# Token sums ahead of the last tile's norm in a hybrid decoder layer on one Trainium2 core

## Chip, core and metric

The kernel runs on one core of a Trainium2 chip. The metric is device time in microseconds for one execution of the whole layer. Five engines take part: TensorE (PE; its weight loads are shown as PEld), VectorE (DVE), ScalarE (ACT), GpSimd (POOL) and SyncE (SP, which here only issues DMA transfers). Each engine works through its own queue in order. An instruction that waits holds up everything behind it on the same engine; engines meet only at semaphores, and so do the DMA transfers.

## What is computed

One layer of a decoder over 1,024 tokens plus 16 meta tokens, model width 1,024, feed-forward width 4,096, float32:

```python
for l in range(DEPTH):                                   # DEPTH = 1
    u = rmsnorm(h, g_pre_mix[l])
    z = u @ w_in[l]
    q, k, v, xr, yr = jnp.split(z, split_at, axis=-1)
    attn = sliding_window_attention_with_sinks(q, k, v, attn_sinks[l])
    xr = causal_depthwise_conv(xr, conv_w[l], conv_b[l])
    hr = rg_lru(xr, ...)
    rec = jax.nn.gelu(yr) * hr
    mix = jnp.concatenate([attn, rec], axis=-1) @ w_out[l]
    h = h + rmsnorm(mix, g_post_mix[l])
    u = rmsnorm(h, g_pre_ffn[l])
    f = jnp.square(jax.nn.relu(u @ w_ff1[l])) @ w_ff2[l]
    h = h + rmsnorm(f, g_post_ffn[l])
return h[:, N_META:]
```

The change touches the place where the output projection (`@ w_out`) ends and the first feed-forward product (`u @ w_ff1`) begins.

## The kernel before

Every float32 product is made of three matmuls (`mm3`, L123 to L133): each operand is split into a high part, rounded to the matmul's format by a copy on ScalarE (L96), and a low part, the rest, from a subtraction on VectorE (L99). `split` (L94) issues both. The three matmuls stand at L125 (high by high), L130 and L131. For a product of a weight tile and a token tile, the third needs the weight's low part and the second that of the tokens, or the other way round. In a row such as `ps_acc<-b,e` the first name is the token operand, the second the weights.

Tiles live in seven pools of equal buffers (`raw` 2, `ws` 5, `a` 16, `b` 17, `c` 8, `d` 4, `e` 2). `slot(tag, ...)` asks for one. A new tile in a pool waits until the last readers of the buffer's former tile are done; so the choice of a pool decides what a load waits for. `a` holds most of the output weights `wo` until the last output projection has been made.

The order on each engine is decided when the program is built: a scheduler takes the calls of the code with their dependences and priorities and may move independent work past each other. `behind(name, ins)` adds an order without a wait. `mark[0]` is the name of the last low part issued.

**Output projection and norms.** Tokens come in eight tiles of 128, `t` = 0 to 7. For each tile `out_mm` makes the projection, `out_norm` (L965) the norm and the residual sum (L972 squares on ScalarE, L978 and L981 on VectorE, the store L982 from SP, L984 the square of the result on ScalarE, L170 and L176 the root on GpSimd), `out_scale` the scaling (L991, VectorE). `u2_tiles` (L994) turns a scaled tile with eight transposes on TensorE (L1003), in two groups of four, and moves them from PSUM to the feed-forward's token operand `u2f`: the first group on ScalarE (L1014, four activations), the second on VectorE (L1008, two operations). Tiles 0 to 3 are half 0 of `u2f`; tiles 4 to 7 are half 1, with its columns in that order.

**Feed-forward, first product.** It is done by seven block products instead of eight (Strassen's scheme, in Winograd's form): weights and tokens are cut into blocks `11`, `12`, `21`, `22`, and sums of blocks are multiplied. The weights come in sixteen stages `p` of 256 columns. `prep_a(p)` loads both halves of a stage (L1026, two transfers of 512 KB from SP's queue, `r0` in pool `raw`, `r1` in `d` or `a`), makes four sums on VectorE (L1029), splits them into `ws` and `e` tiles and stores the last sum to `s_dram` (L1082) from GpSimd's queue. For the first stages some parts of the weights are loaded early by `early` (L1086) into a `raw` tile: block 11 of stages 0 to 3 and block 12 of stages 0 to 3, in pairs. `p1` and `p2` (L1144, L1149) are the two products that need no sum; `p1`'s result is copied on ScalarE (L1147), `p2`'s added on VectorE (L1152). The token sums are `t3` = half-1 block differences and `t2` = `t3` plus half 0 (`t_sums`), with their split operands `ot2` and `ot3`. The products of stage `p` with `ot2` and `ot3` are copied on ScalarE (L1226, L1232). `activate` (L1129) does Relu and Square (L1131, L1132) on a finished block.

**The order around the change.** After the loop over the eight tiles come `p1(0)`, `p1(1)`, `p2(0)`, `p2(1)`; then the token sums of the first three tiles of half 1 in one go (`t_sums(slice(0, 3 * P))`, 768 elements per partition and operation), `prep_a(0)`, the transposes of tile 7, the sums of its columns, `p1(2)`, `p1(3)`, the early load of block 12 for stages 2 and 3 with `p2(2)`, and from there the loop over the sixteen stages: product with `ot2`, `p1(p+2)`, product with `ot3`. `p2(3)` follows the first product with `ot2`. The scheduler puts the transposes of tiles 6 and 7 between matmuls of these products.

Of the kernel before, what the change touches and what calls it, by code (L numbers as in the profile page):

```python
# [11 lines left out]
AF = mybir.ActivationFunctionType  # L12
ALU = mybir.AluOpType
# [3 lines left out]
P = 128  # L17
# [20 lines left out]
def hybrid_layer(  # L38
# [6 lines left out]
    nc = tc.nc  # L45
# [12 lines left out]
    def slot(tag, shape, dt=F32):  # L58
        uid[0] += 1
        return slab.tile(shape, dt, tag=tag, name=f"{tag}{uid[0]}", bufs=bufs[tag])  # L60

    def pair(tag, shape):
        return slot(tag, shape, F32R), slot(tag, shape, F32R)

    def bank(tag, shape=(P, 512)):
        uid[0] += 1
        return ps.tile(list(shape), F32, tag=tag, name=f"ps_{tag}{uid[0]}")

    def f32(ap):
        return ap.bitcast(F32)  # L70
# [23 lines left out]
    def split(hi, lo, src, eng=None):  # L94
        if eng is None:
            nc.scalar.copy(hi, src)  # L96
        else:
            eng.tensor_copy(hi, src)
        low = nc.vector.tensor_tensor(lo, src, f32(hi), op=ALU.subtract).ins  # L99
        mark[0] = low.name  # L100
        return low


    mark = [None]

    def behind(name, *inss):
        for ins in inss:
            tc.add_manual_dep(
                ins, name,
                mybir.DependencyInfo(  # L110
                    mybir.DependencyClass.NoSync, mybir.DependencyReason.DATA
                ),
                reason="order",
            )
# [806 lines left out]
    u2f = [[slot("c", [P, 16, 2, 32]) for _ in range(4)], [None] * 4]  # L921
# [43 lines left out]
    def out_norm(t, po):  # L965
        xr = slot("d", [P, D])
        nc.sync.dma_start(xr, x[t * P : (t + 1) * P, :])
        h = slot("raw", [P, D])
        ssq = [small.tile([P, 1], F32, name=f"sq{n}", tag=f"sq{n}") for n in range(2)]
        for n in range(2):  # L970
            c = slice(512 * n, 512 * n + 512)
            nc.scalar.activation(  # L972
                h[:, c], po[n], AF.Square, scale=RMS_SC, accum_out=ssq[n]
            )
        rs = rstd_of(ssq)
        for n in range(2):
# [4 lines left out]
        summed[t] = nc.vector.tensor_tensor(h, h, xr, op=ALU.add).ins.name  # L981
        nc.sync.dma_start(out[t * P : (t + 1) * P, :], h)  # L982
        ssq2 = small.tile([P, 1], F32, name="ssq", tag="ssq")
        nc.scalar.activation(xr, h, AF.Square, scale=RMS_SC, accum_out=ssq2)  # L984
        return h, xr, rstd_of([ssq2])
# [8 lines left out]
    def u2_tiles(t, xn):  # L994
        half = t // 4
        if u2f[half][0] is None:
            u2f[half] = [slot("c", [P, 2, 512]) for _ in range(4)]
        o = (t % 4) * P
        for k4 in range(0, KC, 4):
            pt = bank("o", (P, 4, P))  # L1000
            for i in range(4):
                kc = k4 + i
                nc.tensor.transpose(pt[:, i, :], xn[:, kc * P : (kc + 1) * P], ident)  # L1003
            for i in range(0, 4, 2):
                kc = k4 + i
                dst = u2f[half][kc // 2]
                if k4:
                    nc.vector.tensor_tensor(  # L1008
                        dst[:, :, o : o + P], pt[:, i : i + 2, :],
                        g_ffn_col[:, kc : kc + 2].to_broadcast([P, 2, P]), op=ALU.mult,  # L1010
                    )
# [16 lines left out]
    def combine(dst, x0, x1, op):  # L1028
        return nc.vector.tensor_tensor(dst, x0, x1, op=op).ins  # L1029

    def rows(t_, c=slice(0, 512)):
        if len(t_.shape) == 4:
            return t_[:, c.start // 32 : c.stop // 32]
        return t_[:, :, c].rearrange("p k (g t) -> p g k t", t=32)
# [48 lines left out]
        return first, (hl[:, 0], hl[:, 1]), (hi[:, :, HI], lo[:, :, HI])  # L1083


    def early(b, p0, hl):  # L1086
        raw = slot("raw", [P, 2, 4, P])
        for k in range(2):
            w1_load(raw[:, k], b, p0 + k, 0, 1)
        split(*hl, raw)  # L1090
        return {p0 + k: (hl[0][:, k], hl[1][:, k]) for k in range(2)}

    a11_early, a12_early = {}, {}
# [34 lines left out]

    def activate(k, q):  # L1129
        t_ = fb[k][q]  # L1130
        nc.scalar.activation(t_, t_, AF.Relu)  # L1131
        return nc.scalar.activation(t_, t_, AF.Square).ins  # L1132

    pos = [out_banks(t) for t in range(4)]
# [7 lines left out]
    ESH = [P, 2, 4, P]  # L1142
# [6 lines left out]
    def p2(p, w, after=None):  # L1149
        y2 = bank("pt")  # L1150
        product(y2, w, b21, True, after)
        nc.vector.tensor_tensor(block("11", p), y2, block("11", p), op=ALU.add)  # L1152

    for t in range(8):
        po = pos[t] if t < 4 else out_banks(t)
        out_mm(t, po, range(6 if t < 4 else 0, KC))
        if t > 5:
            u2_tiles(t - 2, xns[t - 2])
        halfway[t] = out_norm(t, po)
        for k in scale_at[t]:  # L1160
            xns[k] = out_scale(k, *halfway.pop(k))
        if 1 <= t <= 4:
            u2_read(t - 1)
        if t == 7:
            u2_tiles(6, xns[6])
        if t == 4:
            a11_early.update(early(0, 0, pair("a", ESH)))
        if t == 5:
            b11 = operand(u2f[0][0:2])
            a12_early.update(early(1, 0, pair("ws", ESH)))  # L1170
        if t == 6:
            b21 = operand(u2f[0][2:4])
            hl = slot("b", ESH, F32R), slot("e", ESH, F32R)
            a11_early.update(early(0, 2, hl))

    for p in range(2):
        p1(p, a11_early[p])
    for p in range(2):
        p2(p, a12_early[p])
    t3 = [slot("a", [P, 2, 512]) for _ in range(2)]  # L1180
    t2 = [slot("a", [P, 2, 512]) for _ in range(2)]
    ot2 = [pair("b", [P, 2, 512]) for _ in range(2)]

    def t_sums(c):
        for i in range(2):
            combine(t3[i][:, :, c], u2f[1][2 + i][:, :, c], u2f[1][i][:, :, c], ALU.subtract)
            combine(rows(t2[i], c), rows(t3[i], c), rows(u2f[0][i], c), ALU.add)
            hi, lo = ot2[i]
            split(hi[:, :, c], lo[:, :, c], t2[i][:, :, c])

    t_sums(slice(0, 3 * P))
    wa[0] = prep_a(0)
    u2_tiles(7, xns[7])
    t_sums(slice(3 * P, 4 * P))
    urgent = mark[0]
    for p in range(2, 4):
        p1(p, a11_early[p])
    a12_early.update(early(1, 2, pair("a", ESH)))
    p2(2, a12_early[2])
    ot3 = [pair("b", [P, 2, 512]) for _ in range(2)]  # L1200
    for i in range(2):
        behind(urgent, split(*ot3[i], t3[i]))
    wa[1] = prep_a(1, urgent)


# [351 lines left out]
```

## Time and profile before

| | us |
|---|---|
| median of 3 runs (lowest to highest) | 953.0 (952.5 to 953.69) |
| the profiled execution, its own time | 953.17 |
| its span in the profile | 951.5 |
| TensorE busy | 939.7 |
| VectorE busy | 664.5 |
| ScalarE busy | 503.3 |
| GpSimd busy | 135.3 |

The granted TensorE clock is full (0.999) over the span. Times in the views below are microseconds from the start of the span. A row of a timeline gives start, duration, engine, line, operation, tile written and tiles read (without buffer numbers), shape, how many in a row, and in brackets the idle time of the engine before it and what ended it. A row with "x2" shows the duration of both together. TensorE's matmuls are pipelined: each lasts 0.39 us in the record and the next starts while it is under way, so distances between starts matter, not durations. "SPq" rows are the issue of transfers, not the transfers. In the view of waits a row gives the waiting engine, tile and line, who released it, the sum, the number and the longest of such waits. In the windows a row gives, for a stretch of the span, its length, then busy time and number of instructions of PE, PEld, DVE, ACT and POOL, the granted clock, the DMA share and GB/s.

### The profile page before, as it was taken

The numbers are of one execution on the slowest core, as the hardware profiler recorded it, in microseconds if no ns is written. First come the engines' busy times: TensorE is split into PE (matmuls) and PEld (weight loads), VectorE is DVE, ScalarE is ACT, GpSimd is POOL, SyncE is SP. The second block draws the span as 40 slices with busy tenths as digits, with TensorE's granted clock in tenths as the row PEclk, the third lists the DMA queues.
The fourth block names the chain that finished last, engine by engine and source line by source line (L and its number), as shares of the span: only waits on it lengthen the run. The fifth ranks groups of instructions, "written<-read, shape, count | busy, mean of one in ns | idle before, by whom it ended". The sixth has DMA issues, their size and how long they took to land.

```text
span 951.5 us, 12169 instructions
## 1 busy us (share of the span) xinstructions
PE 939.7 (99%) x4584; PEld 785.5 (83%) x4584; DVE 664.5 (70%) x845; ACT 503.3 (53%) x838; POOL 135.3 (14%) x205
## 2 busy tenths in 40 slices
PE   9999999999999999999999999999999999999996
PEld 8999999878888877888888888888888888888885
DVE  6667788779977877665644465476667676779783
ACT  7546765569634554443655585654533343445441
POOL 4104437430021100010000000000121000001201
PEclk9999999999999999999999999999999999999999
DMA  8220011104258567674422364334777755537934
GB/s 272 57 67 23 24 45 45 45 23 145 77 198 267 192 202 243 205 236 148 167 91 89 111 200 131 96 111 127 199 160 179 204 187 186 194 129 210 233 65 89
DMA packets 97366, 134.91 MB, mean 142 GB/s; under 512 B 22230, under 2 KB 61158, under 8 KB 97308
## 3 DMA queue, kind: packets, MB, share of 16 engines
q1 hardware_dynamic: 87996, 108.64, 35.1%
q0 software_dynamic: 8880, 24.19, 12.0%
q10 hardware_dynamic: 432, 1.31, 0.4%
q8 instruction: 36, 0.59, 0.3%
q14 instruction: 22, 0.18, 0.1%
HBM read 112.55 MB, written 20.97 MB: 140 GB/s over the span
## 4 chain that ended last, share of the span: by engine, by line
PE 95%; DMA 2%; DVE 2%; ACT 0%; issue 0%; SPq 0%; DVEq 0%
PE ps_acc L125 11%; PE ps_acc L130 11%; PE ps_acc L131 11%; PE ps_pt L131 6%; PE ps_pt L125 6%; PE ps_pt L130 6%; PE ps_s L131 6%; PE ps_s L125 6%; PE ps_s L130 6%; PE ps_o L125 5%; PE ps_o L130 5%; PE ps_o L131 5%; PE ps_o L697 2%; PE ps_acc L282 1%; PE ps_s L629 1%; PE ps_s L633 1%
## 5 line engine op out<-in xcount | busy, mean ns | idle before, releaser
L99 DVE TENSOR_TENSOR ws<-raw,ws 128x1024 fp32r<-128x1024 f32 (+1 forms) x69 | 82.3, 1193 | 71.3 <-PE ps_o L130 23.1
L96 ACT CAST ws<-raw 128x1024 fp32r<-128x1024 f32 (+1 forms) x68 | 69.7, 1026 | 83.6 <-PE ps_o L130 33.6
L96 ACT CAST ws<-e 128x1024 fp32r<-128x1024 f32 x41 | 43.0, 1049 | 85.6 <-PE ps_o L130 38.2
L130 PE MATMUL ps_acc<-a,ws 128*128 128x512 f32 (+3 forms) x240 | 83.0, 346 | 0.0
L125 PE MATMUL ps_acc<-a,ws 128*128 128x512 f32 (+3 forms) x240 | 82.8, 346 | 0.0
L131 PE MATMUL ps_acc<-a,ws 128*128 128x512 f32 (+3 forms) x240 | 82.2, 343 | 0.0
L99 DVE TENSOR_TENSOR b<-b,b 128x1024 fp32r<-128x1024 f32 (+2 forms) x50 | 59.0, 1179 | 27.9 <-PE ps_o L130 22.7
L96 ACT CAST b<-b 128x1024 fp32r<-128x1024 f32 (+2 forms) x49 | 50.0, 1020 | 42.1 <-DVE b L1029 35.8
L99 DVE TENSOR_TENSOR ws<-e,ws 128x1024 fp32r<-128x1024 f32 x41 | 50.2, 1224 | 30.4 <-ACT ws L96 17.1
L684 POOL TENSOR_SCALAR_AFFINE_SELECT c<-c 128x512 fp32r<-128x512 f32 x64 | 55.0, 873 | 73.7 <-ACT c L96 64.2
L125 PEld LDWEIGHTS ps_acc<-a,ws 128*128 128x128 f32 x240 | 45.2, 189 | 4.3 <-issue 0.7
L131 PEld LDWEIGHTS ps_acc<-a,ws 128*128 128x128 f32 x240 | 45.2, 188 | 3.7 <-issue 0.2
L130 PEld LDWEIGHTS ps_acc<-a,ws 128*128 128x128 f32 x240 | 45.2, 188 | 3.6 <-issue 0.4
L131 PE MATMUL ps_acc<-ws,b 128*128 128x512 f32 (+1 forms) x120 | 46.3, 386 | 0.0
L130 PE MATMUL ps_acc<-ws,b 128*128 128x512 f32 (+1 forms) x120 | 46.2, 385 | 0.0
L125 PE MATMUL ps_acc<-ws,b 128*128 128x512 f32 (+1 forms) x120 | 46.0, 385 | 0.0
L125 PE MATMUL ps_pt<-ws,b 128*128 128x512 f32 x112 | 44.3, 395 | 0.0
L131 PE MATMUL ps_pt<-ws,b 128*128 128x512 f32 x112 | 44.2, 395 | 0.0
L130 PE MATMUL ps_pt<-ws,b 128*128 128x512 f32 x112 | 44.1, 394 | 0.0
L130 PE MATMUL ps_s<-ws,b 128*128 128x512 f32 x110 | 43.4, 395 | 0.0
L131 PE MATMUL ps_s<-ws,b 128*128 128x512 f32 x110 | 43.4, 394 | 0.0
L125 PE MATMUL ps_s<-ws,b 128*128 128x512 f32 x110 | 43.4, 394 | 0.0
(417 smaller groups left out, 2660.3 us busy)
## 6 DMA issues: line engine op xcount, KB each, us to landing
raw<-in_w_ff_dram SPq DMA_DIRECT2D x59, 512.0 KB, 3.9
e<-in_w_ff_dram SPq DMA_DIRECT2D x43, 512.0 KB, 3.2
a<-in_w_ff_dram SPq DMA_DIRECT2D x12, 512.0 KB, 4.9
s_dram<-a POOLq DMA_DIRECT2D x12, 512.0 KB, 3.9
raw<-in_w_in_dram SPq DMA_DIRECT2D x9, 512.0 KB, 3.6
c<-in_x_dram SPq DMA_DIRECT2D x8, 512.0 KB, 5.2
d<-in_x_dram SPq DMA_DIRECT2D x8, 512.0 KB, 3.2
out_dram<-raw SPq DMA_DIRECT2D x8, 512.0 KB
```

The costliest lines, as they stand in the source:

```text
L96: nc.scalar.copy(hi, src)
L99: low = nc.vector.tensor_tensor(lo, src, f32(hi), op=ALU.subtract).ins
L125: ins = nc.tensor.matmul(dst, lh, rh, start=start, stop=False, skip_group_check=True).ins
L130: nc.tensor.matmul(dst, lh, rl, start=False, stop=False, skip_group_check=True)
L131: last_mm[0] = nc.tensor.matmul(dst, ll, rh, start=False, stop=stop, skip_group_check=True).ins.name
L282: last_mm[0] = nc.tensor.matmul(acc[:, :n], w[k // 2][:, kc, :], u[kc][k % 2][:, t0 : t0 + n], start=k == 0 and kc == 0, stop=k == last an ...
L629: nc.tensor.matmul(dst, q[h][:, c], hi, start=True, stop=False, skip_group_check=True,)
L633: nc.tensor.matmul(dst, q[h][:, c], lo, start=False, stop=True, skip_group_check=True,)
L684: nc.gpsimd.affine_select(out=p_[:, :, s], in_=f32(p_[:, :, 0]), pattern=[[0, 4], [g, P]], compare_op=op, fill=0.0, base=0, channel_multip ...
L697: nc.tensor.matmul(two[:, :, oc : oc + w], v, p_.rearrange("p (j i) s c -> p j (i s c)", j=2)[:, :, pc : pc + w], start=n == 0 and k == 0, ...
```

## The change

```diff
@@ u2_tiles
-                if k4:
+                if k4 and t != 6:
                     nc.vector.tensor_tensor(
                         dst[:, :, o : o + P], pt[:, i : i + 2, :],
                         g_ffn_col[:, kc : kc + 2].to_broadcast([P, 2, P]), op=ALU.mult,
@@
-    def early(b, p0, hl):
-        raw = slot("raw", [P, 2, 4, P])
+    def early(b, p0, hl, tag="raw"):
+        raw = slot(tag, [P, 2, 4, P])
@@ activate
-        nc.scalar.activation(t_, t_, AF.Relu)
+        ins = nc.scalar.activation(t_, t_, AF.Relu).ins
+        if k == "11":
+            behind(token_low, ins)
         return nc.scalar.activation(t_, t_, AF.Square).ins
@@
+    def t_sums(c):
+        for i in range(2):
+            combine(t3[i][:, :, c], u2f[1][2 + i][:, :, c], u2f[1][i][:, :, c], ALU.subtract)
+            combine(rows(t2[i], c), rows(t3[i], c), rows(u2f[0][i], c), ALU.add)
+            hi, lo = ot2[i]
+            split(hi[:, :, c], lo[:, :, c], t2[i][:, :, c])
+
     for t in range(8):
...
         if t > 5:
             u2_tiles(t - 2, xns[t - 2])
+        if t == 7:
+            t3 = [slot("a", [P, 2, 512]) for _ in range(2)]
+            t2 = [slot("a", [P, 2, 512]) for _ in range(2)]
+            ot2 = [pair("b", [P, 2, 512]) for _ in range(2)]
         halfway[t] = out_norm(t, po)
...
         if t == 7:
+            t_sums(slice(0, 2 * P))
             u2_tiles(6, xns[6])
@@
+    a12_early.update(early(1, 2, pair("a", ESH), "a"))
     for p in range(2):
         p1(p, a11_early[p])
     for p in range(2):
         p2(p, a12_early[p])
-    t3 = [slot("a", [P, 2, 512]) for _ in range(2)]
-    t2 = [slot("a", [P, 2, 512]) for _ in range(2)]
-    ot2 = [pair("b", [P, 2, 512]) for _ in range(2)]
-
-    def t_sums(c):
-        ...
-    t_sums(slice(0, 3 * P))
+    t_sums(slice(2 * P, 3 * P))
     wa[0] = prep_a(0)
     u2_tiles(7, xns[7])
     t_sums(slice(3 * P, 4 * P))
     urgent = mark[0]
     for p in range(2, 4):
         p1(p, a11_early[p])
-    a12_early.update(early(1, 2, pair("a", ESH)))
     p2(2, a12_early[2])
     ot3 = [pair("b", [P, 2, 512]) for _ in range(2)]
     for i in range(2):
         behind(urgent, split(*ot3[i], t3[i]))
+    token_low = mark[0]
     wa[1] = prep_a(1, urgent)
```

Four things, then. The token sums of tiles 4 and 5 (512 elements per partition and operation) are made inside the last turn of the tile loop, and those of tile 6 (256 elements) later, instead of all three in one piece. The early weights for block 12 of stages 2 and 3 are loaded before the first `p1`, into a buffer of pool `a` instead of `raw`. Relu and Square of each `11` block are ordered behind the low part of the second `ot3` operand. All eight transposes of tile 6 are evicted by ScalarE.

In the built program this also moves the order of neighbouring work. On VectorE the three sums of tiles 4 and 5 stand ahead of tile 6's scaling (L991), the fourth and the first low part ahead of L978 of tile 7, the second low part ahead of L981 of tile 7, and the low part of the early weights right behind it. On TensorE `p1(2)` is no longer interrupted; tile 6's transposes stand four matmuls later, and three matmuls instead of nine lie between tile 7's transposes and `p2(2)`. In SP's queue the early load stands ahead of `r0` of stage 0; `r1` of stage 2 follows that directly; and `r1` of stages 5 and 6 and of 14 and 15 stand behind `r0` of stage 5 and ahead of `r0` of stage 6 (before: `r1` of 5 and 6 ahead of `r0` of 5, `r1` of 14 and 15 behind `r0` of 6). VectorE's first sum of stage 5 stands ahead of the low part of stage 4 (before: behind it). From stage 7 on the orders are the same. The number of transfers and of matmuls is the same.

More of the change, by code (lines that the diff above doesn't have):

```diff
@@ L1179, in hybrid_layer @@
         p2(p, a12_early[p])
-    t3 = [slot("a", [P, 2, 512]) for _ in range(2)]
-    t2 = [slot("a", [P, 2, 512]) for _ in range(2)]
-    ot2 = [pair("b", [P, 2, 512]) for _ in range(2)]
-    def t_sums(c):
[L1185 to L1189, printed above, removed]
-    t_sums(slice(0, 3 * P))
+    t_sums(slice(2 * P, 3 * P))
     wa[0] = prep_a(0)
```

## The prediction

> **What bounds the kernel now.** I read the page first: busy times and the chain that ended last.
>
> ```profile
> span 951.5 us, 12169 instructions
> ...
> PE 939.7 (99%) x4584; PEld 785.5 (83%) x4584; DVE 664.5 (70%) x845; ACT 503.3 (53%) x838; POOL 135.3 (14%) x205
> ...
> PE 95%; DMA 2%; DVE 2%; ACT 0%; issue 0%; SPq 0%; DVEq 0%
> ```
>
> TensorE is the bound from end to end, and the change neither adds nor removes a matmul. It can only move the moments at which TensorE waits. The view of waits for TensorE lists six of them: two in the first microseconds, the other four here (the first and the last of these; all four stand with their brackets in the timeline below).
>
> ```profile
> PE ps_pt L131 <- DVE a L99: 1.0, 1, 1.0
> ...
> PE ps_acc L130 <- DVE b L99: 0.2, 1, 0.2
> ```
>
> These four lie in the change from the output projection to the first feed-forward products. The timeline of TensorE shows where, and gives their full price (start, duration, then the idle time in brackets):
>
> ```profile
> 334.32 0.39 PE L125 MATMUL ps_pt<-b,a 128*128 128x512 f32 x1
> 334.55 0.39 PE L130 MATMUL ps_pt<-b,a 128*128 128x512 f32 x1
> 335.94 0.50 PE L131 MATMUL ps_pt<-b,a 128*128 128x512 f32 x1 [1.00 <-DVE a L99]
> 336.28 0.39 PE L125 MATMUL ps_pt<-b,a 128*128 128x512 f32 x1
> ...
> 338.13 0.39 PE L131 MATMUL ps_pt<-b,a 128*128 128x512 f32 x1
> 338.96 0.50 PE L125 MATMUL ps_acc<-b,e 128*128 128x512 f32 x1 [0.44 <-ACT b L96]
> 339.70 0.50 PE L130 MATMUL ps_acc<-b,e 128*128 128x512 f32 x1 [0.24 <-DVE b L99]
> ...
> 348.93 0.50 PE L131 MATMUL ps_acc<-b,e 128*128 128x512 f32 x1
> ...
> 359.44 0.40 PE L130 MATMUL ps_s<-b,e 128*128 128x512 f32 x1
> 360.39 0.50 PE L131 MATMUL ps_s<-b,e 128*128 128x512 f32 x1 [0.56 <-DVE e L99]
> ...
> 363.34 0.50 PE L131 MATMUL ps_acc<-b,ws 128*128 128x512 f32 x1
> ```
>
> Undisturbed matmuls start 0.23 us apart (334.32 to 334.55), and after a wait the next start is 0.34 later (335.94 to 336.28), 0.11 over. So the four waits cost 335.94-334.55-0.23+0.11 = 1.27, then 0.60, 0.62 and 0.83: 3.3 us, of which 2.5 lie before 340. The matmuls at 348.93 and 363.34, both the first to use a low part, took 0.50 like those after a wait: held up too, too briefly for the list of waits, by some 0.2 each with the 0.11. **3.7 us** is the whole prize, 0.39% of the span.
>
> The windows of 5 us say why (busy time of each engine, clock, DMA share, GB/s):
>
> ```profile
> 325.00:330.00 5.00, 5.00 (x24) 4.04 (x23) 5.00 (x10) 1.79 (x5) 1.49 (x2) 1.00 0.60 168
> 345.00:350.00 5.00, 5.00 (x23) 3.80 (x22) 5.00 (x9) 4.07 (x6) 1.08 (x2) 1.00 0.20 73
> 350.00:355.00 5.00, 5.00 (x23) 4.09 (x22) 0.08 (x1) 1.18 (x2) 0.00 (x0) 1.00 0.99 291
> ```
>
> VectorE has no gap around 325 to 350, and then stands idle for 5 us behind a load. Here, and only here, VectorE's queue sets when TensorE's operands are ready.
>
> **The change part by part.** Its rows on VectorE and ScalarE:
>
> ```profile
> 318.80 0.75 DVE L991 TENSOR_SCALAR d<-raw,rs 128x1024 f32<-128x1024 f32 x1 [1.42 <-POOL rs L176]
> 321.72 1.23 DVE L981 TENSOR_TENSOR raw<-raw,d 128x1024 f32<-128x1024 f32 x1
> 326.00 0.74 DVE L991 TENSOR_SCALAR d<-raw,rs 128x1024 f32<-128x1024 f32 x1
> 334.00 0.75 DVE L1008 TENSOR_TENSOR c<-ps_o,gcol 128x256 f32<-128x256 f32 x2
> 334.67 1.22 DVE L99 TENSOR_TENSOR a<-raw,a 128x1024 fp32r<-128x1024 f32 x1
> 335.80 0.76 DVE L1029 TENSOR_TENSOR a<-c,c 128x256 f32<-128x256 f32 x2
> 336.47 0.96 DVE L99 TENSOR_TENSOR b<-a,b 128x768 fp32r<-128x768 f32 x1
> ...
> 348.19 1.29 DVE L99 TENSOR_TENSOR e<-raw,e 128x512 fp32r<-128x512 f32 x2
> ```
>
> ```profile
> 323.04 1.06 ACT L984 ACTIVATE d<-raw 128x1024 f32<-128x1024 f32 x1 [0.83 <-DVE raw L981]
> ...
> 333.94 1.08 ACT L1131 ACTIVATE d<-d 128x1024 f32<-128x1024 f32 x1
> 334.89 0.84 ACT L96 CAST b<-a 128x768 fp32r<-128x768 f32 x1
> 335.61 1.08 ACT L1132 ACTIVATE d<-d 128x1024 f32<-128x1024 f32 x1
> ```
>
> From start to start an operation on VectorE holds its queue for 0.33 us with 256 elements (335.80 to 336.47 is two), 0.60 with 512 (the two of 348.19 take 1.29, and one alone 0.69, by the row of 355.74 below), 0.87 with 768 (336.47 to the next at 337.34) and 1.13 with 1024 (334.67 to 335.80).
>
> *Token sums.* Six operations of 768 elements (5.2 us) become six of 512 (3.6) and six of 256 (2.0): 0.4 us more. The two evictions of tile 6 that go to ScalarE take off 0.67 (334.00 to 334.67). ScalarE gets them as four more activations, about 1 us, in a window where it is busy 1.79 of 5 us. VectorE's total hardly moves; the place does. VectorE idled 1.42 us before 318.80, and the three sums of tiles 4 and 5 that the new order puts there take 1.9 (one waits on its forerunner), so tile 6's scaling starts at 319.3 instead of 318.80, and tile 7's residual sum (321.72), behind three further pieces, at 323.2: 1.5 late. Who waits for it: ScalarE's square of tile 7 (323.04, now behind the copy of a product, 324.9), GpSimd's root, and VectorE's scaling of tile 7. The last starts 2.96 us after the square now (323.04 to 326.00), so at 327.5 to 327.9. TensorE wants it for tile 7's transposes:
>
> ```profile
> 331.35 1.04 PE L1003 MATMUL ps_o<-ident,d 128*128 128x128 f32 x8
> ```
>
> In the new order three matmuls instead of nine stand between these eight and the product at 334.32, so they come at 334.3-0.7-0.9 = 332.7. Cover for the late scaling: over 4 us; past that, each microsecond late is one of TensorE's.
>
> By "VectorE: DVE Perf Modes" of the Trainium skill (section on the TRN2 errata) every VectorE instruction that reads SBUF pays a fixed cost, some 150 cycles at 0.96 GHz in its measurement, so pieces should hold 512 elements or more. The rows above give 0.06 us for the fixed part (0.33 for 256, 0.60 for 512); by the page the six extra instructions would cost 0.9 us instead of 0.4, an estimate, and half a microsecond would be gone from the room that the last sums have below: the sum would be 0.2 to 0.3 us worse at most.
>
> *Early weights.* The load of the third early pair moves ahead of the first stage's second load and no longer waits in SP's queue for a `raw` buffer:
>
> ```profile
> 326.77 3.04 SPq L1026 DMA_DIRECT2D raw<-in_w_ff_dram  x3
> ...
> 348.90 1.61 SPq L1026 DMA_DIRECT2D raw<-in_w_ff_dram  x2
> 350.56 1.76 SPq L1026 DMA_DIRECT2D a<-in_w_ff_dram  x2
> 360.37 5.42 SPq L1026 DMA_DIRECT2D raw<-in_w_ff_dram  x2
> ```
>
> It was among the three at 326.77; now its buffer is free when the last output projection has ended, so it is issued at about 316.5. Its low part, at 334.67 the thing TensorE waits 1.27 us for, comes at 324.4, ten microseconds before use. It takes 0.5 MB in front of stage 0's second load (issued near 320.1), which VectorE needs by 325.5, when its queue gets there: 5.4 us against a median of 3.9:
>
> ```profile
> raw<-in_w_ff_dram SPq DMA_DIRECT2D x59, 512.0 KB, 3.9
> ```
>
> Were it later than 325.5, VectorE's whole queue would stand behind it, one for one; I take nothing.
>
> *The last tile's sums and the squares.* Relu and Square of the first block (333.94, 335.61, about 1 us each) stood between the casts; now they come behind. I laid the operations in their new order with the durations above. Transposes end at 333.6, VectorE's two evictions start at 333.8, the four sums of 256 end at 336.0, ScalarE's cast for the first operand ends between 336.3 and 336.7, its low part 0.4 later. TensorE, not stopped before, asks at 337.0 and 337.3. Both waits (0.60 and 0.62) go, with 0.2 to 0.6 us to spare.
>
> *What is late next.* TensorE runs 2.5 us earlier, VectorE, laid in the same way, ends its run at 348.4 instead of 350.1: 1.7 earlier. The product of stage 1 starts 48 matmuls after 334.3, at 345.4; its third step, two matmuls of the next product in between, at 346.3 wants a low part that VectorE has ready at 346.6: a new wait of 0.4+0.1 = **0.5**. The load of stage 3 (348.90) can be issued at 346.7, when that low part frees its buffer. Landing 5.5 us later, between 3.9 and the 6.8 shown below, it gives its operands by 356.2, before the product that needs them (48 matmuls and the 0.5 after 345.4: 356.9). The 0.83 goes as well.
>
> *The queue of SP.* In the changed order the loads for stages 5 and 6 (the pair at 350.56) no longer go out ahead of stage 5's first half; they stand behind it, and it waits for stage 3's buffer, freed with that low part at about 356.3. Five loads of 0.5 MB then leave together, with two stores of GpSimd. VectorE's first sum of stage 5, which needs two of them, is queued ahead of the low part of stage 4, wanted by TensorE 86 matmuls and the 0.5 after 345.4, at 365.7. That sum, two more operations of 512 elements and the low part itself come to 2.5 us, so both loads must have landed by 363.2. Nearest row:
>
> ```profile
> 347.97 0.55 POOL L1082 DMA_DIRECT2D s_dram<-d  x1 [19.68 <-DVE d L1029]
> 348.57 0.53 POOL L1082 DMA_DIRECT2D s_dram<-a  x1
> ...
> 355.74 0.69 DVE L1029 TENSOR_TENSOR a<-raw,a 128x512 f32<-128x512 f32 x1 [5.66 <-DMA raw<-in_w_ff_dram]
> ```
>
> The first of four loads, with two stores beside them, was there 6.8 us after its issue at 348.90. I take 7 us from the second issue, 356.8: landing at 363.8, a new wait of 0.6+0.1 = **0.7**. Bounds: nothing (5 us or less, when fewer transfers share) and 5.8 (below). Later stages have no wait in the view above, and the changed program keeps their order.
>
> **Sum**: the 3.7 all go, -3.7 + 0.5 + 0.7 = **-2.5 us**. The profiled execution took 953.17 with its span of 951.5, 0.2 above the median of 953.0: from the median, **950.5**.
>
> **Rivals.** A, the transfer is not late: the first two of the five loads land within 6.4 us of issue, the 0.7 vanishes: 949.8. For it: the median of 3.9; against it: 6.8 at 355.74, with fewer transfers. "DMA: Bandwidth & Descriptors" of the Trainium skill (section on queues, rings and completion order) says that a ring's descriptors are consumed in order; by that rule loads behind cannot slow the first, and A's time would follow. The trace leaves it open, since GpSimd's stores ran beside.
>
> B, both groups are slow: stage 3's load, too, takes 6.8 us, so its low part and stage 4's weights are late by 0.2 and 0.9, and the group of five takes 7 to 8 us from there (0.9 to 1.9): with the 0.5, waits of 2.5 to 3.5 against 3.7 removed: 951.8 to 952.8.
>
> C, the change does not do what it says: tile 7's chain slips by over a microsecond (GpSimd's root, ScalarE's order), and the 0.60 and 0.62 stay: 951.7. Against it: 4 us of cover for the scaling; for it: 0.2 us at the end.
>
> D, slower: the same wait of VectorE's queue at stage 5, with the second load landing only as the whole group is through. Five loads and two stores are 3.7 MB, at the 291 GB/s of 350 to 355 us 12.6 us: 368.9, 5.7 us late, 5.8 of wait: 955.6. It decides from a landing after 366.4, where 3.2 us of wait eat all that is left of the gain.
>
> **How the numbers follow.** Forecast 0.40 (own range 950.0 to 951.1), A 0.22, B 0.20, C 0.08, D 0.10. A measurement of this kernel tells about 0.2%, 1.9 us, from no change: under 951.1 is faster, over 954.9 slower. Faster: forecast, A and an edge, 0.64; slower 0.09, since a part of D stays within; same 0.27. The range 949.6 to 952.8 takes A, the forecast, C and nearly all of B.
>
> **What would show it.** Right: no wait on `a` L99 at p2(2), none on `b` at the first product of the sums; one on `e` L99 near 346 and one near 366; VectorE waiting for a load at about 357 to 364. Wrong: waits on `b` near 337 (C), a VectorE gap reaching past 366 (D), none near 366 (A).

## The result and the profile after

| | before | after |
|---|---|---|
| median (lowest to highest), us | 952.81 (952.5 to 953.69, 6 runs) | 949.15 (948.88 to 949.59, 6 runs) |
| the profiled execution, its own time | 953.17 | 949.03 |
| its span | 951.5 | 947.3 |

The ratio is 0.9961, 95% interval 0.9948 to 0.9974: 3.7 us faster. The prediction had the sign, but the time lies 0.45 us below its range. The page of after begins like that of before:

```profile
span 947.3 us, 12174 instructions
...
PE 937.9 (99%) x4584; PEld 784.8 (83%) x4584; DVE 664.4 (70%) x849; ACT 505.0 (53%) x844; POOL 135.9 (14%) x205
```

The number of matmuls and VectorE's total are as before. The view of waits for TensorE has only the two of the first microseconds left:

```profile
PE ps_acc L309 <- DVE base_e L563: 1.5, 1, 1.5
PE ps_o L358 <- DVE d L248: 0.6, 1, 0.6
```

**Two accounts.** I went through TensorE's timeline from 311 to 400 us and added up what each distance between starts exceeds the undisturbed pace (0.231 us for a matmul of 512 columns, 0.099 for a transpose). This *excess* is 3.97 us before and 0.70 after, so the place of the change gave **3.27 us**. In both, some 0.27 of it stands behind three groups of transposes, which the change does not remove; without them 3.7 became 0.43. What is left after is one short hold (start, duration, operation):

```profile
345.13 0.48 PE L125 MATMUL ps_s<-b,e 128*128 128x512 f32 x1
345.45 0.40 PE L130 MATMUL ps_s<-b,e 128*128 128x512 f32 x1
345.92 0.51 PE L131 MATMUL ps_acc<-b,e 128*128 128x512 f32 x1
346.26 0.40 PE L125 MATMUL ps_acc<-b,e 128*128 128x512 f32 x1
```

The distances 0.32, 0.47 and 0.34 are 0.09, 0.24 and 0.11 over the pace: stage 1's low part, which the prediction had put at 0.5.

The other account is the time up to the change. The chain of waits starts at the first load of the input in both profiles (start and duration); before, then after:

```profile
1.71 5.13 DMA c<-in_x_dram
```

```profile
1.71 4.50 DMA c<-in_x_dram
```

That load landed 0.63 us sooner in the profiled execution of after, and the lead lasted: one and the same matmul, the second of a product just ahead of the change, starts at 316.11 before and at 315.35 after. So 0.76 of the 4.2 us between the two spans arose in code that the change doesn't touch (3.27 + 0.76 = 4.03). Times of after below are therefore compared with those of the prediction by adding 0.76.

VectorE of after, the rows that answer to the prediction's steps (bracket: idle time before and what ended it):

```profile
318.46 0.75 DVE L991 TENSOR_SCALAR d<-raw,rs 128x1024 f32<-128x1024 f32 x1 [0.46 <-POOL rs L176]
...
322.32 1.22 DVE L981 TENSOR_TENSOR raw<-raw,d 128x1024 f32<-128x1024 f32 x1
323.45 1.22 DVE L99 TENSOR_TENSOR a<-a,a 128x1024 fp32r<-128x1024 f32 x1
...
326.76 0.76 DVE L991 TENSOR_SCALAR d<-raw,rs 128x1024 f32<-128x1024 f32 x1 [0.76 <-POOL rs L176]
...
335.63 0.42 DVE L99 TENSOR_TENSOR b<-a,b 128x256 fp32r<-128x256 f32 x1 [0.47 <-ACT b L96]
...
345.18 0.69 DVE L99 TENSOR_TENSOR e<-raw,e 128x512 fp32r<-128x512 f32 x1
345.78 0.69 DVE L1029 TENSOR_TENSOR a<-a,raw 128x512 f32<-128x512 f32 x1
...
346.98 0.69 DVE L99 TENSOR_TENSOR e<-raw,e 128x512 fp32r<-128x512 f32 x1
350.87 0.69 DVE L1029 TENSOR_TENSOR a<-raw,a 128x512 f32<-128x512 f32 x1 [3.20 <-DMA raw<-in_w_ff_dram]
...
361.28 0.69 DVE L1029 TENSOR_TENSOR a<-raw,a 128x512 f32<-128x512 f32 x1 [1.34 <-DMA a<-in_w_ff_dram]
...
363.09 0.69 DVE L99 TENSOR_TENSOR e<-raw,e 128x512 fp32r<-128x512 f32 x1
```

SP's issues of after, and the first two matmuls of stage 4's product, which the forecast stall would have held up at the second low part:

```profile
315.73 1.12 SPq L1026 DMA_DIRECT2D a<-in_w_ff_dram  x2
...
345.89 9.45 SPq L1026 DMA_DIRECT2D raw<-in_w_ff_dram  x3
355.39 1.71 SPq L1026 DMA_DIRECT2D a<-in_w_ff_dram  x2
357.14 1.58 SPq L1026 DMA_DIRECT2D d<-in_w_ff_dram  x2
```

```profile
364.80 0.40 PE L130 MATMUL ps_acc<-b,e 128*128 128x512 f32 x1
365.04 0.40 PE L131 MATMUL ps_acc<-b,e 128*128 128x512 f32 x1
```

The second of the five loads (one at the end of the x3, then the two pairs) is issued at 355.39 and ends VectorE's wait at 361.28: it landed in 5.9 us, not 7. Stage 4's low part (363.09) is done at 363.78, and TensorE asks for it at 365.04. The stall that the prediction priced at 0.7 did not come, with 1.26 us to spare.

### The profile page after: what moved, and what is told of

It is laid out like the page before. It is cut to its first block, busy times and chain, and to the rows that moved or that the text cites. A ratio compares the mean times of both kernels' runs of the same rounds, so it can differ in the third digit from the quotient of the medians.

```text
span 947.3 us, 12174 instructions
## 1 busy us (share of the span) xinstructions
PE 937.9 (99%) x4584; PEld 784.8 (83%) x4584; DVE 664.4 (70%) x849; ACT 505.0 (53%) x844; POOL 135.9 (14%) x205
## 4 chain that ended last, share of the span: by engine, by line
PE 97%; DVE 1%; DMA 0%; ACT 0%; issue 0%; SPq 0%; DVEq 0%
PE ps_acc L125 12%; PE ps_acc L131 12%; PE ps_acc L130 12%; PE ps_pt L131 6%; PE ps_s L131 6%; PE ps_pt L125 6%; PE ps_pt L130 6%; PE ps_s L125 6%; PE ps_s L130 6%; PE ps_o L125 5%; PE ps_o L131 5%; PE ps_o L130 5%; PE ps_o L697 2%; PE ps_acc L282 1%; PE ps_s L629 1%; PE ps_s L633 1%
```

## The experiments

All runs beside the kernel before on the same chip. "Matmul" is the start of that matmul ahead of the change in the profiled execution (a measure of how late the start was), "excess" is TensorE's as above, up to 372 us and from there to 400. The last column is 953.0 minus 3.97 plus the excess, what the time would be if nothing else differed from the kernel before. The kernel before itself had medians of 952.81 to 953.21 us beside them, so the ratios compare better across rows than the medians.

| run | median, us | ratio [95%] | matmul | excess to 372 / to 400 | by the excess |
|---|---|---|---|---|---|
| before | 953.0 | 1 | 316.11 | 3.97 / 0 | 953.0 |
| after, first | 949.15 | 0.9961 [0.9948, 0.9974] | 315.35 | 0.70 / 0 | 949.7 |
| r1 after again | 950.25 | 0.9968 [0.9956, 0.9981] | 315.44 | 0.69 / 0 | 949.7 |
| u1 sums in one piece | 952.04 | 0.9989 [0.998, 0.9998] | 315.47 | 2.80 / 0 | 951.8 |
| u2 weights as before | 951.97 | 0.9989 [0.998, 0.9998] | 315.80 | 2.86 / 0 | 951.9 |
| u3 squares as before | 952.34 | 0.9994 [0.9985, 1.0002] | 316.73 | 2.87 / 0 | 951.9 |
| u4 tile 6 as before | 951.81 | 0.9988 [0.9979, 0.9997] | 315.64 | 2.61 / 0 | 951.6 |
| b1 weights alone | 951.92 | 0.9986 [0.9977, 0.9994] | 315.68 | 3.17 / 0.27 | 952.5 |
| f1 three loads | 951.20 | 0.9981 [0.9972, 0.999] | 316.73 | 0.68 / 1.25 | 951.0 |
| f2 nine loads | 953.78 | 1.0003 [0.9994, 1.0012] | 317.51 | 0.68 / 2.93 | 952.6 |
| x1 stage 1 low first | 950.08 | 0.9964 [0.9951, 0.9976] | 316.00 | 0.85 / 0 | 949.9 |
| o1 after, write first | 951.47 | 0.998 [0.9971, 0.9989] | 315.56 | 2.36 / 0 | 951.4 |
| o2 before, load first | 952.97 | 0.9997 [0.9988, 1.0006] | 315.56 | 3.68 / 0 | 952.7 |
| o3 tile 6, load first | 951.58 | 0.9982 [0.9973, 0.9991] | 316.40 | 2.36 / 0 | 951.4 |
| o4 before, load and cast first | 951.97 | 0.9988 [0.9979, 0.9996] | 315.29 | 2.79 / 0 | 951.8 |
| o5 tile 6, load and cast first | 950.57 | 0.9972 [0.9962, 0.9982] | 315.87 | 1.42 / 0 | 950.5 |

The last column agrees with the median within 0.3 us in ten of the fifteen rows below that of before. It fails for u3 by 0.4, for b1 and the two sets of after by about 0.6, and for f2 by 1.2. The profiled executions do add up: 953.17, the time of that of before, plus the differences in excess and in the start of the matmul, gives the time of each of the other fifteen within 0.35 us. That of f2 (953.97) started 1.40 us later than that of before; whether its other executions did is not recorded.

### The same kernel again

> The changed kernel once more, unaltered, beside the others on one chip. If the 0.76 us that its profiled execution was ahead before 315 us (first load of x landed 4.50 us behind its start, 5.13 before) belongs to the execution and not to the kernel, the profiled start differs again and the median comes out at 949.1 to 949.9, 3.1 to 3.8 us below the kernel before. If it belongs to the kernel, the first load lands at 6.2 us again.

Median 950.25 (949.47 to 951.03, 5 runs): above the interval that was expected by 0.35. The kernel before had 953.21 beside it, not 952.81, so the gain is 2.96 us here and 3.66 in the first set. The excess is the same to 0.01 us. The first load landed 4.68 us after its start, neither 4.50 nor 5.13, and the matmul ahead of the change started at 315.44. This profiled execution was the fastest of the five; what made the other four 0.7 to 1.6 us slower, no trace shows. In o4, whose code up to that place is that of the kernel before, the matmul started at 315.29; in f1 and f2, whose code there is that of after, at 316.73 and 317.51. In all sixteen traces the lead or lag against after is there by 30 us and changes by less than 0.1 us from there to 315. So the start does not come from the code that the change touches. All eleven runs of after together have a median of 949.47; the two sets lie 0.3 us below it and 0.8 above.

### One part of the change undone, or done alone

u1: the sums of all three tiles in one piece, where they were.

```diff
-            t_sums(slice(0, 2 * P))
...
-    t_sums(slice(2 * P, 3 * P))
+    t_sums(slice(0, 3 * P))
```

> The changed kernel with the token sums of tiles 4, 5 and 6 made in one piece again, at their old place; the other three parts stay. Queue theory (VectorE's idle time before 323 us is what the early sums fill): the 3.6 us of sums of 512 elements fall back into the full stretch after 325, while the low part of the early weights (1.1 us) stays out of it. The low part of the third early pair now stands ahead of tile 5's evictions and waits there for its load, some 3 us. So the waits on the sums' operands near 337 come back: 1 to 2 us of waits on b in all, none on a at p2(2), and 950.2 to 951.2 for the time. Rival (the early weights alone made the gain): no wait near 337, 949.0 to 949.4.

u2: the early weights loaded into `raw`, where they were.

```diff
-    a12_early.update(early(1, 2, pair("a", ESH), "a"))
...
+    a12_early.update(early(1, 2, pair("a", ESH)))
     p2(2, a12_early[2])
```

> The changed kernel with the early weights for stages 2 and 3 loaded into a raw buffer at their old place; the other three parts stay. Queue theory: the low part (1.1 us) falls back to about 334 us, and TensorE waits for it at p2(2) as before, 1.0 to 1.3 us; the sums' operands are ready in time because TensorE asks for them that much later. Time 950.0 to 950.6. Rival (the sums alone made the gain): no wait at p2(2), 949.0 to 949.4.

u3: Relu and Square not held behind the sums.

```diff
-        if k == "11":
-            behind(token_low, ins)
```

> The changed kernel without the order of Relu and Square behind the sums' low parts; the other three parts stay. In the built order Relu and Square of the first block then stand ahead of the cast of t3, the cast for the first operand of the sums comes some 1.2 to 1.9 us later, at 336.5 to 337.5 on the changed kernel's clock, and TensorE asks at 336.3. Queue theory: a wait on b at the first product with the sums of 0.5 to 1.5 us, time 949.6 to 950.6. Rival (this order is hidden): none, 949.0 to 949.4.

u4: tile 6's second group evicted on VectorE.

```diff
-                if k4 and t != 6:
+                if k4:
```

> The changed kernel with the second group of tile 6's transposes evicted by VectorE again; the other three parts stay. VectorE gets 0.67 us more work right ahead of tile 7's scaling, where the changed kernel's VectorE stood idle for 0.76 us waiting for GpSimd's root. Queue theory: hidden to 0.3 us, waits of TensorE as in the changed kernel (0.5 us in all) or up to 0.4 more near 337, time 949.1 to 949.6. Rival (each instruction off VectorE counts in full): 0.67 more, 949.8.

b1: the kernel before, with the early weights in pool `a` alone.

```diff
+    a12_early.update(early(1, 2, pair("a", ESH), "a"))
     for p in range(2):
         p1(p, a11_early[p])
...
-    a12_early.update(early(1, 2, pair("a", ESH)))
```

> The kernel before with only the early weights moved and put into pool a; no other part. In the built order their cast and low part stand ahead of tile 5's evictions on ScalarE and VectorE and wait there some 3 us for the load. Queue theory: the 1.27 us at p2(2) go, but VectorE's run up to 350 ends little earlier, so part of it comes back as longer waits on the sums' operands near 337; TensorE's waits between 312 and 400 are 2.5 to 4.0 us (4.0 in the kernel before), time 951.3 to 952.8. Rival (each part brings its own wait's price): 951.5, with the waits on b unchanged at 1.2.

Each of the four undone alone gives back 1.9 to 2.2 us of the 3.27, so that the losses add up to 8.3; and the weights alone gain 0.5 to 1.1 us, less than the 1.27 of the wait that they remove. The parts don't add. The other three were not run alone. In b1 the wait on `a` is gone, TensorE comes earlier to the first product with the sums, and waits there for 1.18 us on ScalarE's cast instead of 0.44. In u2 that wait on `a` is back, on ScalarE's cast first. ScalarE, then TensorE of u2:

```profile
334.61 1.04 ACT L96 CAST a<-raw 128x1024 fp32r<-128x1024 f32 x1 [1.44 <-DMA raw<-in_w_ff_dram]
```

```profile
335.71 0.50 PE L125 MATMUL ps_pt<-b,a 128*128 128x512 f32 x1 [1.53 <-ACT a L96]
```

In u3 the casts of the sums stand behind the Square, as the prediction read it from the profile of before. ScalarE and TensorE of u3:

```profile
336.44 1.10 ACT L1132 ACTIVATE d<-d 128x1024 f32<-128x1024 f32 x1
337.39 2.62 ACT L96 CAST b<-a 128x1024 fp32r<-128x1024 f32 x4
```

```profile
338.82 0.50 PE L125 MATMUL ps_acc<-b,e 128*128 128x512 f32 x1 [0.93 <-ACT b L96]
```

u4 shows what the two evictions are worth. They take VectorE 0.67 us, and in u4 its queue has the addition of `p2(2)`, which waits for TensorE, ahead of the sums' last low parts; in after, one of these (335.63 above) goes in front of it. VectorE and TensorE of u4:

```profile
336.83 0.69 DVE L1154 TENSOR_TENSOR b<-ps_pt,b 128x512 f32<-128x512 f32 x1 [0.68 <-PE ps_pt L131]
337.44 1.89 DVE L99 TENSOR_TENSOR b<-a,b 128x256 fp32r<-128x256 f32 x3
```

```profile
337.91 0.50 PE L130 MATMUL ps_acc<-b,e 128*128 128x512 f32 x1 [0.82 <-DVE b L99]
```

That is 1.05 us of excess. A second loss is common to u1, u3, u4 and b1: the wait on `e` near 360, gone in after and in u2, is there with 0.5 to 0.7 us and its small neighbours. The last group of runs goes into it.

### Does a load wait for those behind it?

f1: the loads of stages 14 and 15 held back until stage 7's first, so that three loads leave together at stage 5 and not five.

```diff
+        if p > 13:
+            behind(r0_load[7], ins)
```

> The changed kernel with the loads for stages 14 and 15 ordered behind stage 7's first load: three transfers instead of five leave SP's queue when stage 3's buffer comes free. The prediction's step (loads behind slow those ahead): the second load, which VectorE waits for at 361.3, lands 1 to 2 us earlier than the 5.9 us after its issue of the changed kernel. Ring order (loads behind cannot slow the first): it lands within 0.4 us of 5.9. Either way TensorE has no wait there; the time is 949.0 to 949.4.

f2: four more transfers of 512 KB, from weights to a scratch area in DRAM that nothing reads, right behind the load in question: nine.

```diff
+        if p == 5:
+            for n in range(4):
+                more = nc.sync.dma_start(more_dram[n], w1v[0][:, :, 256 * (11 + n) : 256 * (12 + n)]).ins
+                behind(ins.name, more)
```

> The changed kernel with four more transfers of 512 KB, from the weights to unused memory, in SP's queue right behind the first two of the five loads for stages 5 and later: nine instead of five. It computes nothing more. The prediction's step: the second load lands 2 us or more later than the 5.9 us after its issue, and TensorE waits at stage 4's low part for 1 us or more. Ring order: it lands within 0.5 us of 5.9, no wait near 365; only what stands behind, the loads of stage 6, comes later, with waits there of 0 to 3 us.

SP and VectorE of f1 (the load, and the sum that waits for it), then of f2:

```profile
356.73 1.69 SPq L1026 DMA_DIRECT2D a<-in_w_ff_dram  x2
```

```profile
362.31 0.69 DVE L1029 TENSOR_TENSOR a<-raw,a 128x512 f32<-128x512 f32 x1 [0.98 <-DMA a<-in_w_ff_dram]
```

```profile
357.54 0.67 SPq L1026 DMA_DIRECT2D a<-in_w_ff_dram  x1
358.26 4.12 SPq L1069 DMA_DIRECT2D more_dram<-in_w_ff_dram  x4
...
366.42 4.12 SPq L1026 DMA_DIRECT2D raw<-in_w_ff_dram  x2
```

```profile
363.43 0.69 DVE L1029 TENSOR_TENSOR a<-raw,a 128x512 f32<-128x512 f32 x1 [1.33 <-DMA a<-in_w_ff_dram]
...
377.63 0.69 DVE L1029 TENSOR_TENSOR a<-raw,a 128x512 f32<-128x512 f32 x1 [6.35 <-DMA raw<-in_w_ff_dram]
```

From issue to the end of the wait: 5.58 us with three loads, 5.89 with five (after), 5.89 with nine. The loads behind do not slow it by more than 0.31 us, and four more cost nothing. Those behind the added transfers are late instead: VectorE idles 6.35 us at stage 6, TensorE waits 2.18 us near 380, and the kernel loses all it had gained. In f1 a wait of TensorE for ScalarE, 0.98 us, came near 389, where the order of the later loads had changed. This settles the prediction's rivals A and D. The Trainium skill, "DMA: Bandwidth & Descriptors" (section on queues, rings and completion order), says that each DMA engine takes a ring's descriptors in order; the traces agree, with 5.89 us for five loads and for nine.

### Stage 1's low part first

x1: in stage 1, the `e` operand's sum and low part ahead of the other low part, for the 0.43 us that are left.

```diff
+        if p == 1:
...
+            low = split(hl[:, 0], hl[:, 1], a11).name
+            behind(low, split(hi[:, :, HI], lo[:, :, HI], a21))
```

> The changed kernel with the low part of stage 1's sum (the e tile) made ahead of the low part of its other half (the ws tile). The wait of 0.24 us and its two delays of 0.1 near 345.9 go: TensorE's waits between 312 and 397 fall from 0.7 to 0.3, which is what the transposes show in any case. Queue theory: 0.4 us faster than the changed kernel, 948.6 to 949.0, too little to tell from it by the times alone. Rival (something else is late by as much): the wait moves to the next low part, 949.1.

The hold near 346 shrank from 0.44 to 0.30 us beyond the pace, but small ones of 0.11 and 0.18 us came back near 357 and 360; with the 0.27 of the transposes 0.85 in all. Its 950.08 can't be told from after. With 0.43 us left at this place, another order of it can gain no more than that, less than the two sets of after differ by.

### Which order brings the wait on `e` back?

In u1, u3, u4 and b1, as in the kernel before, VectorE makes stage 2's last sum ahead of stage 1's low part; in after and in u2 it is the other way round (345.18 and 345.78 above). The sum releases GpSimd's second store to DRAM; the low part frees the `raw` buffer, and so releases stage 3's load. GpSimd, SP and VectorE of u4:

```profile
346.77 0.53 POOL L1082 DMA_DIRECT2D s_dram<-a  x1
```

```profile
347.11 1.62 SPq L1026 DMA_DIRECT2D raw<-in_w_ff_dram  x2
```

```profile
353.92 0.69 DVE L1029 TENSOR_TENSOR a<-raw,a 128x512 f32<-128x512 f32 x1 [5.63 <-DMA raw<-in_w_ff_dram]
```

The load landed 6.81 us after its issue; in after 4.98 (345.89 to 350.87), with the second store issued behind it:

```profile
346.76 0.53 POOL L1082 DMA_DIRECT2D s_dram<-a  x1 [0.65 <-DVE a L1029]
```

Three runs ask for the swap of the two instructions alone. o1 puts after's into the order of before; o2 and o3 put those of before and of u4 into the order of after.

```diff
-        split(hl[:, 0], hl[:, 1], a11)
-        combine(a12, a12, a11, ALU.subtract)
+        e_low[p] = split(hl[:, 0], hl[:, 1], a11)
+        a12_sum = combine(a12, a12, a11, ALU.subtract)
+        if p == 2:
+            behind(e_low[1].name, a12_sum)
```

(In o1 the last line is `behind(a12_sum.name, e_low[1])`.)

> The changed kernel, with VectorE's low part of stage 1 (which frees a raw buffer) put behind stage 2's sum (which starts the second 512 KB write to DRAM), as the kernel before has these two; nothing else is asked for, but the order of the later loads comes back to that of the kernel before with it. In the traces so far stage 3's load landed 4.98, 4.99, 4.94, 4.97 and 4.67 us behind its issue where that lay ahead of the second write, and 6.84, 6.94, 6.79, 6.81 and 6.92 where it lay behind it. Theory (the load queues behind the write): issue some 0.6 us later, landing 6.8 to 6.9 us behind it, a wait of 0.5 to 0.8 us of TensorE at stage 3's low part near 359, and 0.5 to 0.8 us more than the changed kernel of this call. Rival (it landed early for another reason, the later order of SP's queue): landing 5.0 and no more than 0.2 us of difference.

> The kernel before with one pair of VectorE's instructions swapped: stage 1's low part ahead of stage 2's sum, so that stage 3's load is issued ahead of the second write. Theory: the load is issued 0.6 us earlier and lands 5.0 us behind its issue (6.84 before), TensorE's wait of 0.56 us on e near 360 goes, and the kernel runs 0.6 to 0.8 us faster than before (about 952.3); the waits of 1.0, 0.44 and 0.24 us at 335 to 340 stay. Rival (four loads in a bunch share the engines): it lands 6.8 us behind its issue, and the wait shrinks only by the 0.6 us of the earlier issue.

> The changed kernel with tile 6's evictions as before, and the same pair of VectorE's instructions put in the changed kernel's order (stage 1's low part ahead of stage 2's sum). Theory: of the 1.9 us that the changed kernel loses with tile 6's evictions as before, the load's part (a wait of 0.55 us at 358.6 and its small one behind it) comes back: 0.6 to 0.8 us faster than that run, 951.0 to 951.2; the wait of 0.82 us on b near 337.9 stays, since its cause is the two evictions on VectorE. Rival (the evictions cost it all): no difference.

GpSimd, SP and VectorE of o1:

```profile
346.36 0.53 POOL L1086 DMA_DIRECT2D s_dram<-a  x1
```

```profile
346.69 11.95 SPq L1026 DMA_DIRECT2D raw<-in_w_ff_dram  x3
```

```profile
353.63 0.69 DVE L1029 TENSOR_TENSOR a<-raw,a 128x512 f32<-128x512 f32 x1 [5.77 <-DMA raw<-in_w_ff_dram]
```

The landing follows the order each time: 6.94 us in o1 (346.69 to 353.63), 4.94 in o2 (347.75 to 352.69), 4.93 in o3. Two other things move with the swap. The next load in SP's queue follows 1.20 to 1.24 us behind in o1 and before, 1.80 to 1.85 in after and o2; but f1 and f2 show that a load behind matters little. And the load is issued 0.93 us behind the first store in o1, 0.33 in after; but in x1 it is 0.96, with the second store issued behind the load, and it landed in 4.67. So the second store is left. The transfers of the profile show it at work: in o1, from 346.5 to 350.5 us, the two stores' packets (1.04 MB) take 83% of the DMA engines' time, and only 0.08 MB of the load's 0.52 moves beside them; it lands 3.1 us after that.

TensorE's wait did not follow. In o1 it came back as expected, 0.63 us at 358.3, and the run cost more than expected, 1.2 us against r1 (1.67 in the excess), since the swap also made stage 1's low part 0.6 us later, for which TensorE waits already. But in o2 and o3 a wait of 0.47 us stayed, and o2 gained nothing that can be measured. VectorE and ScalarE of o2:

```profile
352.69 0.69 DVE L1029 TENSOR_TENSOR a<-raw,a 128x512 f32<-128x512 f32 x1 [3.15 <-DMA raw<-in_w_ff_dram]
...
357.02 0.69 DVE L99 TENSOR_TENSOR ws<-raw,ws 128x512 fp32r<-128x512 f32 x1 [2.19 <-ACT ws L96]
```

```profile
355.89 0.59 ACT L1236 COPY a<-ps_acc 128x512 f32<-128x512 f32 x1 [2.19 <-PE ps_acc L131]
356.37 0.62 ACT L96 CAST ws<-raw 128x512 fp32r<-128x512 f32 x1
```

The load lands 1.9 us sooner after its issue than in before, but VectorE now waits 2.19 us for the cast, and the cast stands behind an eviction that waits 2.19 us for TensorE. With the swap, the built order had taken these two the other way round (before: cast at 357.19, eviction at 357.71). o4 and o5 are o2 and o3 with that eviction behind the casts:

```diff
-        nc.scalar.copy(block("21", p), ya[p])
+        ins = nc.scalar.copy(block("21", p), ya[p]).ins
+        if p == 1:
+            behind(e_cast, ins)
```

> The kernel before with the swap of run o2 (stage 3's load ahead of the second write) and one more: ScalarE's eviction of stage 1's second product, which waits for TensorE until 355.9 us, is put behind the two casts of stage 3. In run o2 the load landed 1.9 us earlier, but the cast stood behind that eviction (cast at 356.37, its operand summed by 354.8), and TensorE's wait at stage 3's low part stayed at 0.47 us. Theory (the wait passed from the load to ScalarE's queue): casts at 354.2 to 355.5, stage 3's low part done by 357.6, asked for at 358.9; the wait of 0.47 and its small neighbours (0.64 + 0.06 beyond the pace) go, and the run is 0.6 to 0.8 us faster than o2 (952.97), so 952.2 to 952.4. Rival (VectorE's queue holds it: stage 4's sum, which stands ahead of stage 3's low part and waits for stage 4's load): the wait stays at 0.3 us or more.

> The changed kernel with tile 6's evictions as before (the load first as in run o3), and the same order on ScalarE: the eviction behind stage 3's two casts. Theory: TensorE's wait of 0.47 us at 359 goes, what stays against the changed kernel is the wait on b near 338 (0.31 + 0.75 us beyond the pace in o3, 0.05 to 0.1 in the changed kernel), and the run is 0.6 to 0.8 us faster than o3 (951.58), so 950.8 to 951.0. Rival: as in o4, no difference.

ScalarE of o4, and its waits of TensorE:

```profile
353.89 0.62 ACT L96 CAST ws<-raw 128x512 fp32r<-128x512 f32 x1 [0.40 <-DVE raw L1029]
354.61 0.62 ACT L96 CAST e<-raw 128x512 fp32r<-128x512 f32 x1
355.69 0.59 ACT L1238 COPY a<-ps_acc 128x512 f32<-128x512 f32 x1 [0.45 <-PE ps_acc L131]
```

```profile
PE ps_pt L131 <- DVE a L99: 1.0, 1, 1.0
...
PE ps_acc L125 <- ACT b L96: 0.4, 1, 0.4
PE ps_acc L130 <- DVE b L99: 0.3, 1, 0.3
```

The wait on `e` is gone in both. The excess fell by 0.89 (o2 to o4) and 0.94 us (o3 to o5), the time by 1.0 and 1.0 (951.97 after 952.97, 950.57 after 951.58; these were not run side by side, so the two figures of the traces weigh more). Shown, then: the load ahead of the store does not remove that wait by itself, and with the cast ahead of the eviction it does. The cast alone was not moved in any run; in before VectorE's row from the landing (355.74) to stage 3's low part (359.66) has no gap, and the cast that this low part reads was done 0.85 us before, so there the load held it. After has both (350.87 above; the casts of stage 3 at 352.32 and 353.05, the eviction at 353.63). What u4 loses apart from it is the 1.05 near 338, still there in o5.

## Why the prediction was right or wrong

- **TensorE as the bound, and the 3.7 us prize.** Right: without the transposes there were 3.69 us of excess before, and all but 0.2 us of the rest of the difference between the two profiles is their start.
- **The first three waits go** (1.27, 0.60, 0.62). Right, by the steps laid out. With 0.76 added: the early load issued at 316.5 (316.5 forecast), its low part at 324.2 (324.4), tile 6's scaling 319.2 (319.3), tile 7's residual sum 323.1 (323.2), its scaling 327.5 (327.5 to 327.9). Rival C fell.
- **The 0.83 goes.** Right in its result: VectorE's run ends at 348.43 (348.4) and stage 3's load is issued at 346.65 (346.7). The landing was set at 5.5, between bounds, and was 4.98; why one or the other holds was not seen. The runs showed it: whether GpSimd's second store goes first. The first half of rival B is this case with the store first: o1, with 6.94 us for stage 3's load, had 951.47. Its second half, 7 to 8 us for the group of five, came in no run (5.8 to 6.0 us in after, r1, u2 and o1).
- **A new 0.5 at stage 1's low part.** Right: 0.43 to 0.44, asked for at 346.4 (346.3 forecast) and ready at 346.6 (346.6).
- **A new 0.7 at stage 4's low part.** Wrong: this is the step that failed, "I take 7 us from the second issue, 356.8: landing at 363.8". The load was issued at 356.15 on that clock and landed 5.89 us later, at 362.04; needed by 363.2. Of the 1.76 us, 1.1 come from the landing and 0.65 from the earlier issue. The nearest row, 6.8 us at 355.74, was no measure of how many loads share a queue: it was a load behind two stores, and the prediction put two stores beside the five loads as well; in after one store (354.03) stood ahead of them, and the next was issued at 362.99, after the landing. Rival A, with 949.8, is what happened.
- **The sum.** With that term at nothing it is -3.7 + 0.43 = -3.27, measured -3.27 in the excess: 949.7 from 953.0. The two sets of after, 949.15 and 950.25, lie on either side of it. The range began 0.2 us under rival A, less than the 1.1 us between the two sets of this kernel, so that the first set fell below it.
- **Fixed cost of small pieces on VectorE.** No wait arose where the six extra instructions went; VectorE's run ended to 0.03 us where the rows' durations had put it.

## What to carry to other kernels

When loads queue on one engine, price a landing by what is ahead of it, in its own queue and in the others, and not by what is behind; for a row that serves as the price, ask what stood in front of that one. When several waits follow each other on one path, removing one partly moves the engine on to the next: here the one part that was run alone gained 0.5 to 1.1 us, and each part taken out of the whole cost 1.9 to 2.2 of 3.27. And where an order is built by a scheduler, look for a wait's second holder (here an eviction ahead of a cast) before giving the first one its price.

## What the runs showed of the hardware

- A load of 512 KB in SP's queue landed 4.67 to 4.99 us after its issue when it was issued ahead of GpSimd's second store (ten runs), and 6.79 to 6.94 when it was issued behind it (six runs). The 1.9 us are about the time of one such transfer at the 291 GB/s that before shows for 350 to 355 us (0.524 MB: 1.8 us, an estimate). The two are in different queues. The same page of the Trainium skill says in the same section that a DMA engine takes turns between the queues it has work for; the trace agrees: in o1, from 348.7 to 350.5 us, GpSimd's queue moved 94 packets and SP's 75. Here the turns went by packets, not by bytes: these were 0.39 MB of the stores, in packets of 4 KB, and 0.08 MB of the load, in packets of 1 KB. So the load got on only when the stores were nearly through.
- What stood behind a load in its own queue made little or no difference: 5.58, 5.89 and 5.89 us to land as the second of three, five and nine.
- The start moves by up to 2.2 us between the profiled executions (315.29 to 317.51 us for one and the same matmul, which stands ahead of the change). The landing of the first load has up to 0.7 us of this (4.41 to 5.13 us in the seven profiles whose chain begins with it); in f2, the latest, 1.5 us more arise between 21 and 30 us, with a wait of TensorE for ScalarE of 0.73 us at 23.5 that after doesn't have.
